# Two gate vectors summed by matrix products, and three masked-matrix steps on GpSimd, in a one-core hybrid layer

## The chip, the core and the metric

One core of a Trainium2 chip runs the whole program. The metric is the device time of one execution in microseconds (us). The core's engines work side by side, each with its own instruction stream: TensorE (PE) for matrix products, VectorE (DVE), ScalarE (ACT) and GpSimd (POOL) for elementwise work. The DMA transfers of this kernel are issued from the queue of SyncE (SP), in order.

## The reference, cut to what matters

The reference is one layer of a generator over 1024 latent tokens of 1024 features, with 256 context tokens. Six vectors of 1024 (shift, scale and gate, twice) come from the conditioning vector:

```python
m = jax.nn.silu(cvec) @ w_ada + b_ada         # 1024 x 6144
sh1, sc1, g1, sh2, sc2, g2 = jnp.split(m, 6)
u = modulate(x, sh1, sc1) @ w_in              # z, x|B|C, dt, f, p
# scan over chunks of 128 tokens, 8 heads, two directions
dt = softplus(dt_raw + dt_bias);  dA = -dt * exp(a_log);  cs = cumsum(dA)
y_diag = einsum("bclhn,bcshn,bhcls,bcshp->bclhp", C, B, exp(segsum(dA)), x * dt)
y = y_diag + (C @ states) * exp(cs)
y = group_rms_norm((y + x * d_skip) * silu(z)) * norm_w
x = LN(alpha * x + g1 * (concat(y, fourier(f), pool(p)) @ w_out))
x = LN(alpha * x + g2 * conv_ffn(modulate(x, sh2, sc2)))
```

Convolution (three taps) and silu go ahead of x, B and C. The term `y_diag` needs, for every chunk and head, the masked matrix of `C B^T` times the decay between two tokens times `dt`, in both directions. A group of four heads shares `B` and `C`; there are two groups.

## The kernel before, in words

Products run in a 32-bit format of TensorE that keeps fewer bits, so each operand is split into a high and a low part, and a product takes three passes.

**Stages.** To 98 us: loads, the layer norm of the tokens, the first shift and scale, and z. From 98 to 228: eight *blocks* of the input projection, in the order B4, C6, B5, C7, x0, x1, x2, x3, 128 columns each, 48 products (L433). Then two blocks for the Fourier part (`pf0`, `pf1`), two for pooling (`pp0`, `pp1`), the scan's outputs by chunk (`Y`, to about 395), the output projection (`pout`, 343 to 467), and the feed-forward net, whose products start at 514 us. The change touches the part from 98 to 395.

**A block** (`block_a`, L553; `block_b`, L573): 48 products and, for B and x, 24 short ones for the context (L444); the convolution, one ACT pass and two on DVE (L548 to L550); silu on ACT (L551); then, in the middle of the next block, transposes on TensorE (`tt`, L578) and copies of them by ACT and DVE (L584, L589), which free PSUM. PSUM is held as two tiles of two banks for the blocks and four of one bank, in rotation, for all else (`tt`, `pc`, `pg`, `pada` and so on).

**The six vectors.** The first shift and scale come early. The other four are made in 32 *pieces* (`ada_piece`, L379): piece i is a load of 128 rows by 1024 columns of `w_ada` (tile `wad`, 512 KB), and DVE multiplies it with the column of silu(c) and adds it to an accumulator of 128x1024 (`aacc`, L389). Pieces 0 to 15 give g1 and sh2, 16 to 31 sc2 and g2. `ada_rows(j)` (L391) sums an accumulator's 128 partitions by four products with a matrix of ones, each into its own 32 rows of one PSUM bank (`pada`, four column groups, L396), copies the result by ACT (`arw`, L398) and stores it. The list `pieces((4, 6, 1, 1, 8, 0, 0, 0)[bi])` says how many pieces come after each block; 12 came before the first.

**The sixteen masked matrices** (`chunk_pre`, L600): one for each chunk and group, in the order of chunks 4, 5, 6, 7, 3, 2, 1, 0 with group 0 and then again with group 1, three after each block from C7 on. The name of a tile has chunk and group: EU30 is chunk 3, group 0, the fifth made. For each:

- TensorE: `pg` = B C^T (L604). DVE: `gt`, both triangles of it (L608).
- DVE: `U` = upper triangle times `dt` (L610, 128x512); then for each of four heads `U` += lower triangle times the other `dt` (L631, 128x128).
- SP: two loads `bc` of the cumulated decays, broadcast over the partitions (L617, from `cs_scratch`); there are two such tiles. POOL (group 0, L619) or ACT (group 1, L623) and ACT again (L628) subtract the own decay; DVE takes the minimum (L630 in group 0, L625 in group 1).
- ACT: the exponential (L632). POOL: times `U` (L633). SP: the store (L634, `m_scratch`).

E and U of a matrix are the two halves of one tile `EU`. Later `Y(i)` (L931) loads a chunk's matrix and states, makes the products, and normalises: two ACT sums of squares (L908), a logarithm and an exponential on two elements a row (`sr`, L911 and L912), a Newton step on DVE (`ssn_t`, L137 to L141), the scaling (L919), transposes on TensorE (`pyt`, L924). A logarithm-and-exponential table set is loaded for it by one instruction of its own (L1009); other table loads go in where an activation needs another set.

**The order.** The calls above say what is computed; a scheduler at build time lays the instructions of each engine into one fixed order, by its own estimates of when operands are ready. An engine never overtakes in that order, and SP's queue doesn't either.

Of the kernel before, what the change touches and what calls it, by code (L numbers as in the profile page):

```python
# [8 lines left out]
F32 = mybir.dt.float32  # L9
F32R = mybir.dt.float32r  # L10
AF = mybir.ActivationFunctionType
ALU = mybir.AluOpType
# [14 lines left out]
def rev_ap(t, hi, n):  # L27
    """Free elements hi, hi-1, ... (n of them) of a two-dimensional tile or AP."""
    a = t[:, hi : hi + 1]
    return bass.AP(a.tensor, a.offset, [list(a.ap[0]), [-1, n]])  # L30
# [3 lines left out]
def hybrid_layer(  # L34
# [16 lines left out]
    def open_psum(na, nb):  # L51
        """PSUM as na tiles of two banks and nb of one."""
# [17 lines left out]
    # Memory that is handed from stage to stage: tags of [P, 1024] words.  # L70
# [11 lines left out]
    def half(tag, name, shape=(P, 512), dt=F32):  # L82
        """One of two tiles of 512 words of a tag of the small pool."""
        return sl.tile(list(shape), dt, tag=tag, name=name, bufs=2)
# [26 lines left out]
    # columns: c 0:8, c_ctx 8:16, conv w 16:40 (tap*8+tile), conv b 40:48, norm_w 48:52, pool_scale 52:54,  # L111
    # b_ada of the first shift 54:62 and scale 62:70
# [21 lines left out]
    def newton(r, v, n, name):  # L134
        """One Newton step of r towards 1/sqrt(v)."""
# [8 lines left out]
    def rstd(var, n, name, scale=1.0):  # L144
        """1/sqrt(var*scale + eps): square root, reciprocal, one Newton step."""
# [8 lines left out]
    def ln_stats(srcs, name):  # L154
        """Mean, 1/deviation and -mean/deviation of the rows of several token tiles, [P, tiles] each."""
# [12 lines left out]
    def modulate(xns, c0, c1, sc, sh, hi, lo, tmps, lo_eng, name, via_act=False):  # L168
        """Transpose token tiles, scale and shift per feature, split into two parts; hi and lo are functions of a range
        of feature tiles."""  # L170
# [33 lines left out]
    def split(raw, hi, lo, eng=None):  # L204
        """hi = raw rounded to float32r, lo = raw - hi (exact)."""
# [3 lines left out]
    # ================= mixer =================  # L209
# [8 lines left out]
    def wblock(c0, name, tags=None):  # L218
        """128 columns of w_in in two parts."""
# [8 lines left out]
    def zload(j, q):  # L228
        """Half the rows of 264 columns: dt and z[0:248], or z[248:512]."""
# [17 lines left out]
    def load_wa(qd):  # L247
        """A quarter of the shift's and of the scale's columns."""
# [28 lines left out]
    hh = [htile("H0", "hh0"), htile("H1", "hh1")]  # L277
    hl = [htile("H2", "hl0"), htile("H3", "hl1")]
    ada1 = sl.tile([P, 2, 8, 2], F32, name="ada1")  # shift or scale, feature tile, latents or context

    def ada_quarter(qd):
        """Two feature tiles of the first shift and scale, for latents and context."""
# [1105 lines left out]
```

## Time and profile before

| | us |
|---|---|
| runs, three | 1237.48, 1238.14, 1640.35; median 1238.14 |
| profiled execution, first to last instruction (span) | 1238.0 |
| TensorE busy in it | 1159.4 (94%) |
| DVE busy | 988.0 (80%) |
| POOL busy | 467.0 (38%) |
| ACT busy | 375.3 (30%) |

The page gives the profiled execution no time of its own beside the span; the span is 0.1 below the median of the runs. Views of the trace list, for a stretch of time, the busy time of each engine; for a group of instructions, their number, total and mean (or shortest, median and longest, in ns); for a wait, who waited, what released it, the total, the number of times and the longest. In a timeline row stand start, duration, engine, line, operation, and in brackets the idle time before it with what ended it. Busy time of an engine that nothing waits for costs nothing; a busy engine that TensorE waits for costs all of it.

### The profile page before, as it was taken

What the parts mean: (1) busy time and instruction counts of PE and PEld (TensorE: products, weight loads), DVE (VectorE), ACT (ScalarE), POOL (GpSimd) and SP (SyncE); (2) the same over time, 40 slices, a digit from 0 to 9 for tenths busy, and PEclk for the clock granted to TensorE, in tenths of its full rate; (3) what the DMA queues carried; (4) which work ended last, traced back from release to release, by engine and by line L of the source; (5) the groups of instructions that cost most, each with busy time, mean ns of one, the idle gap of its engine ahead of it and who ended that gap; (6) DMA issues with size and microseconds to landing.
All of it is one profiled execution on the core that took longest, in us unless ns stands there. A gap on an engine that the chain in (4) does not pass through costs nothing.

```text
span 1238.0 us, 14349 instructions
## 1 busy us (share of the span) xinstructions
PE 1159.4 (94%) x5463; PEld 943.4 (76%) x5463; DVE 988.0 (80%) x1426; ACT 375.3 (30%) x559; POOL 467.0 (38%) x243
## 2 busy tenths in 40 slices
PE   4999998889978998999999999999999999999992
PEld 2798877768756886788888888888888888888881
DVE  4788799999898889798777777777777777778958
ACT  2263566712344132432222212222212122222140
POOL 0010143353352033575353435353434344353254
PEclk9999998989889998999999999999999999999996
DMA  9848555556624011221110212110211112011012
GB/s 314 293 146 298 169 159 173 167 198 219 221 77 171 33 35 51 86 68 51 34 55 31 69 34 68 35 52 34 68 34 50 53 34 69 27 58 52 2 50 119
DMA packets 104637, 122.52 MB, mean 99 GB/s; under 512 B 7006, under 2 KB 83564, under 8 KB 104568
## 3 DMA queue, kind: packets, MB, share of 16 engines
q1 hardware_dynamic: 104567, 121.60, 30.3%
q8 instruction: 43, 0.70, 0.2%
q14 instruction: 27, 0.21, 0.1%
HBM read 106.82 MB, written 14.76 MB: 98 GB/s over the span
## 4 chain that ended last, share of the span: by engine, by line
PE 74%; DVE 16%; DMA 4%; issue 3%; ACT 1%; POOL 1%; SPq 0%; DVEq 0%; ACTq 0%; POOLq 0%
PE pu L1219 37%; PE pdn L1144 16%; PE pout L994 4%; PE px L433 4%; PE pz L332 4%; PE pl L1266 2%; DMA bc<-cs_scratch 1%; PE pu L1180 1%; DVE EU L631 1%; DMA wa<-in_w_ada_dram 1%; DVE pn_st L161 1%; DVE st L696 1%; PE pp L433 1%; DVE xa L1063 1%; PE pd L896 1%
## 5 line engine op out<-in xcount | busy, mean ns | idle before, releaser
L1170 DVE SCALAR_TENSOR_TENSOR cv<-pu,ffc,cv 128x945 f32<-128x945 f32 (+7 forms) x368 | 432.6, 1177 | 20.5 <-ACT cv L1162 10.7
L1219 PE MATMUL pu<-h2h,wul 128*128 128x512 f32 x656 | 205.5, 394 | 0.0
L1219 PE MATMUL pu<-h2h,wuh 128*128 128x512 f32 x656 | 205.2, 394 | 0.0
L1219 PE MATMUL pu<-h2l,wuh 128*128 128x512 f32 x656 | 204.5, 393 | 0.0
L1147 DVE TENSOR_TENSOR xa<-xa,pdn 128x512 f32<-128x512 f32 x128 | 87.4, 683 | 128.9 <-PE pdn L1144 128.6
L207 POOL TENSOR_TENSOR wul<-wur,wuh 128x1024 fp32r<-128x1024 f32 x44 | 106.0, 2409 | 207.9 <-ACT wuh L206 207.9
L1219 PEld LDWEIGHTS pu<-h2h,wuh 128*128 128x128 f32 x656 | 123.3, 188 | 28.9
L1219 PEld LDWEIGHTS pu<-h2l,wuh 128*128 128x128 f32 x656 | 123.3, 188 | 28.6
L1219 PEld LDWEIGHTS pu<-h2h,wul 128*128 128x128 f32 x656 | 123.3, 188 | 27.8
L206 ACT ACTIVATE wuh<-wur 128x1024 fp32r<-128x1024 f32 x44 | 46.3, 1054 | 237.1 <-PE pu L1219 221.5
L1144 PE MATMUL pdn<-wdh,gl 128*128 128x512 f32 x288 | 113.3, 394 | 0.0
L1144 PE MATMUL pdn<-wdl,gh 128*128 128x512 f32 x288 | 113.3, 393 | 0.0
L1144 PE MATMUL pdn<-wdh,gh 128*128 128x512 f32 x288 | 113.1, 393 | 0.0
L1242 POOL TENSOR_TENSOR wdr<-wdr,g2b 128x1024 f32<-128x1024 f32 x22 | 53.0, 2411 | 68.4 <-DMA wdr<-in_ffn_w_down_dram 68.4
L1238 POOL TENSOR_TENSOR cv<-cv,cv 128x1024 f32<-128x1024 f32 (+1 forms) x23 | 53.1, 2308 | 60.5 <-ACT cv L1237 60.4
L207 POOL TENSOR_TENSOR gl<-cv,gh 128x1024 fp32r<-128x1024 f32 (+1 forms) x23 | 53.4, 2320 | 42.3 <-ACT gh L206 42.3
L1144 PEld LDWEIGHTS pdn<-wdh,gh 128*128 128x128 f32 x288 | 54.1, 188 | 12.9
L1144 PEld LDWEIGHTS pdn<-wdh,gl 128*128 128x128 f32 x288 | 54.1, 188 | 12.4
L1144 PEld LDWEIGHTS pdn<-wdl,gh 128*128 128x128 f32 x288 | 54.1, 188 | 12.2
L1162 ACT ACTIVATE cv<-pu,ffc 128x1024 f32<-128x1024 f32 (+3 forms) x46 | 53.1, 1154 | 29.0 <-PE pu L1219 18.8
L1237 ACT ACTIVATE cv<-cv 128x1024 f32<-128x1024 f32 (+1 forms) x23 | 23.5, 1022 | 120.6 <-DVE cv L1170 120.6
L207 POOL TENSOR_TENSOR wdl<-wdr,wdh 128x1024 fp32r<-128x1024 f32 x22 | 52.8, 2414 | 4.7 <-ACT wdh L206 4.7
(348 smaller groups left out, 2142.9 us busy)
## 6 DMA issues: line engine op xcount, KB each, us to landing
wur<-in_ffn_w_up_dram SPq DMA_DIRECT2D x44, 512.0 KB
wad<-in_w_ada_dram SPq DMA_DIRECT2D x32, 512.0 KB
wdr<-in_ffn_w_down_dram SPq DMA_DIRECT2D x22, 512.0 KB
wa<-in_w_ada_dram SPq DMA_DIRECT2D x32, 256.0 KB
bc<-cs_scratch SPq DMA_DIRECT2D x32, 256.0 KB
xr<-in_x_dram SPq DMA_DIRECT2D x8, 512.0 KB
wx_r<-in_w_in_dram SPq DMA_DIRECT2D x8, 512.0 KB
m_scratch<-EU SPq DMA_DIRECT2D x16, 256.0 KB
```

The lines of the kernel that those rows point to most:

```text
L206: S.activation(hi, raw, AF.Identity)
L207: (eng or G).tensor_tensor(lo, raw, hi.bitcast(F32), op=ALU.subtract)
L332: TE.matmul(pt[:, j * 512 : j * 512 + ZW], a, b[:, k % 4, :], start=first and i == 0, stop=last and i == 2)
L433: TE.matmul(pt[:, q * 512 : q * 512 + 512], a[:, k, :], b[q][:, k, :], start=k == 0 and i == 0, stop=k == KD - 1 and i == 2)
L994: TE.matmul(pt[:, nb * 512 : nb * 512 + 512], u, v[:, nb * 512 : nb * 512 + 512], start=first and i == 0, stop=last and i == 2)
L1144: TE.matmul(pt, u_, v_[:, s], start=i == 0, stop=i == n - 1)
L1147: V.tensor_tensor(xa[t][:, s], xa[t][:, s], pt, op=ALU.add)
L1162: S.activation(acc[:, a * 64 : b * 64], pt[:, a * 64 : b * 64], AF.Identity, bias=ffc[:, 396 + ct : 397 + ct], scale=ffc[:, 176 + ct : 177 ...
L1170: last = V.scalar_tensor_tensor(dst, pv[:, r0 + dy : r1 + dy, c0 + dx : c1 + dx], ffc[:, w * 44 + ct : w * 44 + ct + 1], dst, op0=ALU.mult ...
L1219: TE.matmul(pt[:, q * 512 : q * 512 + 512], a[:, k, :], b[q][:, k, :], start=k == 0 and j == 0, stop=k == KD - 1 and j == 2)
L1238: G.tensor_tensor(acc[:, s], acc[:, s], acc_v[:, s], op=ALU.mult)
L1242: G.tensor_tensor(raw, raw, g2b, op=ALU.mult)
```

## The change

**First**, pieces 16 to 31 (j = 1) are no longer accumulated on DVE. Two loaded pieces with the same rows are multiplied at once on TensorE: four products of 32 columns (silu(c) of these rows, for both vectors and padding) with 512 columns, one in each column group, accumulating over the eight pairs in one PSUM bank `pada1`, which stays taken from the first pair to `ada_rows(1)`. The bias is loaded into row 0 of each group of a tile `abias`; DVE adds it when the sum is read. The pieces follow the blocks as 4, 6, 4, 6, and `ada_rows(1)` stands in block x0 instead of x2. **Second**, in `chunk_pre` the product with `dt` is made by GpSimd: `U` as before, `ub` for the lower triangle in one operation, and their sum. `gt` has two buffers. **Third**, the builder reserves less memory for dynamic DMA. The diff removes comments and docstrings besides, so line numbers move.

```diff
     def ada_piece(i):
         j, kk, q = i // 16, (i % 16) // 2, i % 2
         o = 2048 + j * 2048 + q * 1024
-        if i % 16 < 2:
+        if j == 0 and i < 2:
             aacc[j, q] = qt(f"q{6 + q}", f"aacc{j}{q}")
             G.memset(aacc[j, q], 0.0)
             nc.sync.dma_start(aacc[j, q][0:1, :], b_ada[0:1, o : o + 1024])
         t = qt(ptags[i], f"wad{i}")
         nc.sync.dma_start(t, w_ada[kk * P : (kk + 1) * P, o : o + 1024])
-        av = aacc[j, q][:]
-        V.scalar_tensor_tensor(av, t, sil[:, kk, 0:1], av, op0=ALU.mult, op1=ALU.add)
+        if j == 0:
+            av = aacc[j, q][:]
+            V.scalar_tensor_tensor(av, t, sil[:, kk, 0:1], av, op0=ALU.mult, op1=ALU.add)
+            return
+        if kk == 0:
+            aacc[j, q] = t
+            if q == 0:
+                aacc["bias"] = sl.tile([P, 512], F32, name="abias")
+                G.memset(aacc["bias"], 0.0)
+                for b in range(4):
+                    nc.sync.dma_start(aacc["bias"][32 * b : 32 * b + 1, :], b_ada[0:1, o + b * 512 : o + b * 512 + 512])
+                aacc["sum"] = psb("pada1")
+        aacc[j, q] = t
+        if q == 1:
+            for b in range(4):
+                TE.matmul(aacc["sum"][32 * b : 32 * b + 32, :], sil[:, kk, :],
+                          aacc[j, b // 2][:, (b % 2) * 512 : (b % 2) * 512 + 512], start=kk == 0, stop=kk == KD - 1)
 
     def ada_rows(j):
         assert npiece[0] >= 16 * (j + 1)
-        pt = psb(f"pada{j}")
         arw = half("xw", f"arw{j}")
-        for b in range(4):
-            TE.matmul(pt[32 * b : 32 * b + 32, :], ones[:, 0:32], aacc[j, b // 2][:, (b % 2) * 512 : (b % 2) * 512 + 512],
-                      start=True, stop=True)
-        S.copy(arw, pt)
+        if j == 0:
+            pt = psb(f"pada{j}")
+            for b in range(4):
+                TE.matmul(pt[32 * b : 32 * b + 32, :], ones[:, 0:32],
+                          aacc[j, b // 2][:, (b % 2) * 512 : (b % 2) * 512 + 512], start=True, stop=True)
+            S.copy(arw, pt)
+        else:
+            V.tensor_tensor(arw, aacc["sum"], aacc["bias"], op=ALU.add)
...
     def chunk_pre(ch, g):
...
-        gt = sl.tile([P, 2, P], F32, tag="gt", name=f"gt{ch}{g}")
+        gt = sl.tile([P, 2, P], F32, tag="gt", name=f"gt{ch}{g}", bufs=2)
         V.tensor_tensor(gt, pg[:, 0:P].unsqueeze(1).broadcast_to([P, 2, P]), t12, op=ALU.mult)
         f = g * 8
-        V.tensor_tensor(U, gt[:, 0, :].unsqueeze(1).broadcast_to([P, 4, P]),
+        G.tensor_tensor(U, gt[:, 0, :].unsqueeze(1).broadcast_to([P, 4, P]),
                         dtv[:, ch, f : f + 4].unsqueeze(2).broadcast_to([P, 4, P]), op=ALU.mult)
+        ub = sl.tile([P, 4, P], F32, tag="ub", name=f"ub{ch}{g}", bufs=2)
+        G.tensor_tensor(ub, gt[:, 1, :].unsqueeze(1).broadcast_to([P, 4, P]),
+                        dtv[:, ch, f + 4 : f + 8].unsqueeze(2).broadcast_to([P, 4, P]), op=ALU.mult)
         for h in range(4):
...
-            V.scalar_tensor_tensor(U[:, h, :], gt[:, 1, :], dtv[:, ch, b : b + 1], U[:, h, :], op0=ALU.mult, op1=ALU.add)
+        G.tensor_tensor(U, U, ub, op=ALU.add)
         S.activation(E, E, AF.Exp)
         G.tensor_tensor(U, U, E, op=ALU.mult)
...
-        if bi in (1, 6):
+        if bi in (1, 4):
             mids[3].append(lambda: ada_rows(bi // 4))
...
-        pieces((4, 6, 1, 1, 8, 0, 0, 0)[bi])
+        pieces((4, 6, 4, 6, 0, 0, 0, 0)[bi])
...
+    nc = _bacc.Bacc("TRN2", target_bir_lowering=False, num_devices=1, dynamic_dma_scratch_size=1024)
```

With other work to lay out, the scheduler orders three engines differently in places. Names carry a number at their end that tells buffers apart.

SP's queue during block x0, where the stores of the first three matrices (EU40, EU50, EU60) and the `bc` loads of the following ones are issued. Before:

```order
L617 DMA bc700_1707<-cs_scratch 128x2x256
L634 DMA m_scratch<-EU40_1535 128x512
L222 DMA wx3_r_1988<-in_w_in_dram 128x8x128
L617 DMA bc702_1715<-cs_scratch 128x2x256
L634 DMA m_scratch<-EU50_1560 128x512
L634 DMA m_scratch<-EU60_1585 128x512
L617 DMA bc300_1732<-cs_scratch 128x2x256
L617 DMA bc302_1740<-cs_scratch 128x2x256
L634 DMA m_scratch<-EU70_1703 128x512
L617 DMA bc200_1757<-cs_scratch 128x2x256
```

Now:

```order
L640 DMA bc702_1759<-cs_scratch 128x2x256
L222 DMA wx3_r_2002<-in_w_in_dram 128x8x128
L657 DMA m_scratch<-EU40_1555 128x512
L657 DMA m_scratch<-EU50_1579 128x512
L420 DMA ada_scratch<-arw1_1704 1x512
L657 DMA m_scratch<-EU60_1603 128x512
L420 DMA ada_scratch<-arw1_1704 1x512 x3
L640 DMA bc300_1777<-cs_scratch 128x2x256
L640 DMA bc302_1783<-cs_scratch 128x2x256
L640 DMA bc200_1801<-cs_scratch 128x2x256
L640 DMA bc202_1807<-cs_scratch 128x2x256
L640 DMA bc100_1938<-cs_scratch 128x2x256
```

The loads for the fifth, sixth and seventh matrix now come in one run, all behind the first three stores and the store of the second gate sums; the loads of the fifth stand behind the third store in both. The store of the fourth matrix follows them instead of dividing them.

DVE around the convolution of block x0 (`cv0`; its four rows of L549 and L550 before are L569 and L570 now). Before:

```order
L610 TENSOR_TENSOR EU60_1585<-gt60_1586,dtv_1067 128x512
L549 SCALAR_TENSOR_TENSOR cv0_1666<-px0_1617,col_94,cv0_1666 128x1023
L631 SCALAR_TENSOR_TENSOR EU60_1585<-gt60_1586,dtv_1067,EU60_1585 128x128 x4
L550 SCALAR_TENSOR_TENSOR cv0_1666<-px0_1617,col_94,cv0_1666 128x1023
L549 SCALAR_TENSOR_TENSOR cvc0_1696<-pc0_1667,col_94,cvc0_1696 128x255
```

Now, with the copies of the transposes of x0 at the end:

```order
L653 TENSOR_TENSOR EU30_1771<-EU30_1771,bc300_1777 128x256
L653 TENSOR_TENSOR EU30_1771<-EU30_1771,bc302_1783 128x256
L569 SCALAR_TENSOR_TENSOR cv0_1710<-px0_1655,col_94,cv0_1710 128x1023
L653 TENSOR_TENSOR EU20_1795<-EU20_1795,bc200_1801 128x256
L570 SCALAR_TENSOR_TENSOR cv0_1710<-px0_1655,col_94,cv0_1710 128x1023
...
L653 TENSOR_TENSOR EU10_1932<-EU10_1932,bc100_1938 128x256
L653 TENSOR_TENSOR EU10_1932<-EU10_1932,bc102_1944 128x256
L604 COPY xt1_1871<-tt00_1860 128x2x128
L614 COPY xtc_1874<-ttc0_1879 128x2x128
L604 COPY xt3_1873<-tt01_1861 128x2x128
```

The minima of the fifth matrix (EU30) stood behind x0's convolution and now stand ahead of it, and those of the seventh (EU10) ahead of the copies of x0's transposes.

ACT at the last silu, that of block x3 (`cv3`). Before:

```order
L551 ACT_TABLE_LOAD
L551 ACTIVATE cv3_2255<-cv3_2255 128x1024
L551 ACTIVATE cvc3_2285<-cvc3_2285 128x256
...
L632 ACT_TABLE_LOAD
L632 ACTIVATE EU31_2292<-EU31_2292 128x512
L1009 ACT_TABLE_LOAD
```

Now, with the first chunk's normalisation, which had L911 and L912 side by side before:

```order
L1032 ACT_TABLE_LOAD
...
L571 ACT_TABLE_LOAD
L571 ACTIVATE cv3_2255<-cv3_2255 128x1024
...
L655 ACT_TABLE_LOAD
L655 ACTIVATE EU21_2354<-EU21_2354 128x512
...
L934 ACT_TABLE_LOAD
L934 ACTIVATE sr4_2805<-ss4_2802,epsc_97 128x2
L935 ACT_TABLE_LOAD
L935 ACTIVATE sr4_2805<-sr4_2805 128x2
```

The load of the table set for logarithm and exponential (L1009, now L1032) has moved from behind the last silu to ahead of it, and each of the eight chunks now has two table loads in its normalisation; the whole listing of ACT has 40 table loads instead of 24.

More of the change, by code (lines that the diff above doesn't have):

```diff
@@ L1371 @@
     from concourse.bass_utils import run_bass_kernel_spmd as _run
-    nc = _bacc.Bacc("TRN2", target_bir_lowering=False, num_devices=1)
+    nc = _bacc.Bacc("TRN2", target_bir_lowering=False, num_devices=1, dynamic_dma_scratch_size=1024)
     arrays, args = {}, []
```

## Prediction

> **What bounds the kernel now.** I read the page first (engine shares, the chain that ended last), then busy time by stretches, then the waits of the stretch that the change touches, then the start of each projection block on TensorE.
>
> ```profile
> span 1238.0 us, 14349 instructions
> PE 74%; DVE 16%; DMA 4%; issue 3%; ACT 1%; POOL 1%; SPq 0%; DVEq 0%; ACTq 0%; POOLq 0%
> ```
>
> TensorE carries the whole program; DVE comes next with 16% of the chain. The second view shows where. Its columns are stretch, length, then busy us of PE, PEld, DVE, ACT and POOL, the granted clock, the DMA share and GB/s.
>
> ```profile
> 125.00:170.00 45.00, 45.00 (x230) 37.05 (x229) 37.67 (x53) 26.33 (x39) 12.86 (x12) 1.00 0.61 188
> 150.00:290.00 140.00, 126.39 (x616) 104.04 (x615) 131.53 (x251) 70.26 (x127) 59.10 (x52) 0.95 0.57 180
> 180.00:190.00 10.00, 6.41 (x34) 5.53 (x33) 8.91 (x16) 3.85 (x10) 6.34 (x5) 0.82 0.54 161
> 190.00:200.00 10.00, 9.71 (x46) 8.32 (x46) 8.03 (x15) 5.72 (x12) 3.08 (x4) 0.84 0.54 159
> 260.00:270.00 10.00, 6.84 (x27) 5.31 (x26) 9.94 (x28) 1.91 (x5) 3.66 (x3) 0.75 0.41 137
> 270.00:280.00 10.00, 8.88 (x36) 7.05 (x36) 7.61 (x11) 1.53 (x2) 6.18 (x5) 0.91 0.46 157
> ```
>
> From 125 to 170 PE has no gap. From 150 to 290, where the masked matrices are made, PE is idle for 13.6 us (140 less 126.39), DVE is 94% busy and POOL 42%. The lowered clock costs some more: 18% of 6.41, 16% of 9.71, 25% of 6.84 and 9% of 8.88 make 5.2 us. So a DVE with nothing to do there could give back at most about 19 us of 1238; 2% of the time (25 us, about what a measurement of this kernel can tell from no change) is out of reach from this stage.
>
> The third view is the waits: engine, line, releaser, us in total, times, longest.
>
> ```profile
> SPq L634 <- POOL EU L633: 39.1, 15, 5.0
> POOL EU L619 <- DMA bc<-cs_scratch: 35.9, 11, 8.3
> ```
>
> This is a ring: SP's queue stands at the store of a masked matrix until POOL's multiplication L633 is done, the next `bc` load is behind it in that queue, and POOL waits for that load at L619. Today the ring has slack, since POOL is 42% busy. Where TensorE's blocks start:
>
> ```profile
> 156.97 0.72 PE L433 MATMUL px<-hh,wx_h 128*128 128x512 f32 x2
> 171.60 0.71 PE L433 MATMUL px<-hh,wx_h 128*128 128x512 f32 x2
> 193.20 0.73 PE L433 MATMUL px<-hh,wx_h 128*128 128x512 f32 x2
> L433 PE MATMUL pp<-hh,wp_h x24: 388/396/582, 276.3 to 307.7; 128*128 128x512 f32 x24
> ```
>
> x0, x1 and x2 start at 157.0, 171.6 and 193.2, pp0 at 276.3. An undisturbed block is 14.6 us (x0 to x1).
>
> **The change part by part.** Prices:
>
> ```profile
> L389 DVE SCALAR_TENSOR_TENSOR aacc<-wad,sil,aacc 128x1024 f32<-128x1024 f32 x29 | 37.5, 1311 | 3.2 <-DMA wad<-in_w_ada_dram 3.2
> L610 DVE TENSOR_TENSOR EU<-gt,dtv 128x512 f32<-128x512 f32 x16 | 14.4, 898 | 0.1
> L631 DVE SCALAR_TENSOR_TENSOR EU<-gt,dtv,EU 128x128 f32<-128x128 f32 x64 | 23.7, 409 | 0.1
> L633 POOL TENSOR_TENSOR EU<-EU 128x512 f32<-128x512 f32 x16 | 23.5, 1469 | 30.4 <-ACT EU L632 17.8 <-issue 10.0 <-DVE EU L631 2.5
> L633 POOL TENSOR_TENSOR EU<-EU x16: 1279/1297/2206, 165.2 to 269.3; 128x512 f32<-128x512 f32 x16
> L669 POOL TENSOR_TENSOR xw<-xt,wdec x14: 1037/1145/2017, 246.4 to 282.3; 128x512 f32<-128x512 f32 x14
> L619 POOL TENSOR_TENSOR EU<-bc,ncs x16: 612/640/1995, 143.5 to 206.1; 128x256 f32<-128x256 f32 x16
> 129.05 1.00 PE pada L396 x8
> 187.64 0.58 PE L444 MATMUL pc<-hch,wx_h 128*128 128x256 f32 x1 [3.59 <-DVE gt L608]
> ```
>
> *DVE* loses 16 x 1.31 = 21.0 us of L389, 14.4 of L610 and 23.7 of L631: 59 us, nearly all between 130 and 290.
>
> *PE* gains eight groups of four column-group products. The one group that the trace shows (pada, eight records) took 1.0 us; eight of them less the one dropped make +7 us: three near 130, two near 147, three behind the `pg` products ahead of x0. PE has no gap there, so none is hidden: x0 starts at about 165. Bounds 0 (if a later gap takes them up) and 7. The sum also holds one of the four one-bank PSUM tiles until DVE has added the bias, at about 165. The last row shows the dearest wait of PE for such a tile, 3.6 us until DVE had read the `pg` in it, but that was with DVE full; from 130 to 165 DVE loses work, so I take nothing, bounds 0 and 3.6.
>
> *The bias and the sum* go from an ACT copy to a DVE addition on as many elements, and one memset and four small loads move to before 100 us, where SP only queues weights: nothing. Issuing pieces 23 to 31 earlier puts more 512 KB loads into 140 to 165, ahead of the `bc` loads of the second and third matrix; POOL then waits at L619, but its new work starts only at 162, so that too is nothing. The smaller DMA scratch frees memory and costs nothing: the page lists no queue that would use it.
>
> *POOL* gains three 128x512 operations for each of the 16 matrices (8 chunks, 2 groups). No row shows these forms. Two have a broadcast operand, as L669 has (1.145 median), one adds two full tiles, as L633 multiplies them (1.297). Bounds 1.145 and the mean of L633, 1.47; I walk with 1.28, that row's shortest, since the two broadcast forms are nearer to L669. That is 61 us more, and per matrix two L619 and four big operations, 2 x 0.64 + 4 x 1.28 = 6.4 us. Three matrices go with one block: 19.2 us of POOL against 14.6 of PE. So the slack is gone, and POOL sets the pace of the x blocks if anything waits for it. The order listing says that something does: on DVE, x0's convolution stands behind the two minima of the fifth matrix (EU30); the copies that free PSUM ahead of x2 stand behind both minima of the seventh (EU10); and x3's convolution behind those of the thirteenth (EU31). On SP, `bc` of the fifth is behind the stores of the first three.
>
> ```profile
> 156.44 4.13 DMA bc<-cs_scratch
> 184.12 0.33 SPq L634 DMA_DIRECT2D m_scratch<-EU  x1
> 184.56 0.37 SPq L617 DMA_DIRECT2D bc<-cs_scratch  x1
> 172.10 1.27 DVE L549 SCALAR_TENSOR_TENSOR cv<-px,col,cv 128x1023 f32<-128x1023 f32 x1
> 134.87 1.28 ACT L551 ACT_TABLE_LOAD   x1 [2.03 <-DVE cT L550]
> 136.16 1.06 ACT L551 ACTIVATE cT<-cT 128x1024 f32<-128x1024 f32 x1
> ```
>
> The walk, which holds PE's 7 us too: POOL starts batch one at 162 (the `gt` tiles follow `pg` at about 161.5). Twelve big operations and two L619 take 16.6: third multiplication done at 178.8. Store and load issue (0.33 + 0.37) and 4 us for landing: `bc` of the fifth matrix at 183.5. Two L619 and a minimum: 185. Two convolution passes and what stands between, 3 us; table load and silu, 2.3: x0's transposes at about 191. Batch two starts on POOL when its `gt` are made, 189.5; eleven big operations and two L619 later (204.9) the copies ahead of x2 may go, and x2 starts at 207 instead of 193.2, 14 us late. The blocks behind it keep that distance (pp0 at 290 against 276): the last batches hold fewer matrices to a block. With the broadcast forms at 1.145, some 16 of them on this path, 2 us come off. **Term one: +12 us**, with bounds -12 (DVE was all that held PE: 19 back, 7 paid) and +25 (1.47 for the 48 big operations of four batches, 0.19 x 48 = 9 more, and the 3.6 of the PSUM tile).
>
> *The table loads.* The diff doesn't name this. Before, the order has the load of the logarithm-and-exponential set (L1009) behind the last silu. Now it stands ahead of it, silu throws it out, and every chunk's Ln and Exp of the group norm (L911, L912) reload: 16 loads of 1.28 us, 20.5 us on ACT between 297 and 395.
>
> ```profile
> 238.27 1.28 ACT L1009 ACT_TABLE_LOAD   x1
> L912 ACT ACTIVATE sr<-sr x8: 188/204/223, 300.1 to 394.3; 128x2 f32<-128x2 f32 x8
> 300.08 0.20 ACT L912 ACTIVATE sr<-sr 128x2 f32<-128x2 f32 x1
> 300.44 0.15 DVE L137 TENSOR_TENSOR ssn_t<-sr 128x2 f32<-128x2 f32 x1
> 320.09 0.16 DVE L137 TENSOR_TENSOR ssn_t<-sr 128x2 f32<-128x2 f32 x1 [0.39 <-ACT sr L912]
> 381.43 0.16 DVE L137 TENSOR_TENSOR ssn_t<-sr 128x2 f32<-128x2 f32 x1 [0.39 <-ACT sr L912]
> 300.00:310.00 10.00, 10.00 (x57) 8.60 (x56) 9.94 (x16) 5.83 (x16) 4.14 (x2) 1.00 0.44 157
> ```
>
> A pair of loads makes a chunk's `sr` 2.6 us later. The chunks at 320 and 381 wait for `sr` already, with PE's transposition behind DVE: 5.1 us in full. In the first chunk DVE came 0.16 us after `sr`, so it would stand 2.4 us; PE had other work then (10.00 busy in 300 to 310), so of the first two I count half, 2.4. The fourth and sixth have some 1.5 us of DVE work in hand and pay 1 each; the fifth and eighth are covered by DVE's and PE's own work. **Term two: +9.5 us**, bounds 5.1 and 20.5. The Trainium skill, "ScalarE: Activation LUTs", section "What ACT_TABLE_LOAD costs", gives 2.66 us for a switch, load and drain. By it ACT would pay 42.6 us, and term two would be twice as large, 1269 in all; in the row at 136.16 the activation starts right behind its 1.28 us load, so the trace doesn't bear the drain out.
>
> Sum: 1238.0 + 12 + 9.5 = 1259.5; the median of the runs shown is 0.1 above the span, and I say **1259**. The forecast's own range is 1250 to 1269.
>
> **The rivals.** *R1, DVE's relief wins.* If the convolutions don't wait for POOL because the 59 us let everything arrive earlier, PE runs without gaps: -19 + 7, and 5 for the tables (the lower bound): 1231. For it: DVE's 94%. It decides where a batch of POOL fits into 14.6 us, which takes (14.6 - 6 x 0.64)/12 = 0.90 us an operation, under every row above, or where PE's blocks have enough in hand not to need what POOL holds up. *R2, POOL is absorbed.* It paces nothing though it leaves DVE no gain either, and 2 of PE's 7 us are not taken up by the gaps: 1238 + 2 + 9.5 = 1249. For it: POOL waited up to 8.3 us for the ring's loads, and the longest stop of PE in these blocks was the 3.6 at 187.64.
>
> *R3, the two engines block each other.* DVE operations with two inputs in SBUF stretch beside POOL:
>
> ```profile
> 372.01 2.76 DVE L905 TENSOR_TENSOR y<-y,z 128x512 f32<-128x512 f32 x1
> 317.81 0.69 DVE L905 TENSOR_TENSOR y<-y,z 128x512 f32<-128x512 f32 x1
> 182.87 1.50 DVE L630 TENSOR_TENSOR EU<-EU,bc 128x256 f32<-128x256 f32 x1 [0.51 <-POOL EU L619]
> 189.51 0.42 DVE L630 TENSOR_TENSOR EU<-EU,bc 128x256 f32<-128x256 f32 x1 [0.58 <-ACT bc L628]
> ```
>
> The same L905 took 2.76 and 0.69: 2.07 more. With POOL nearly always busy, the two minima (L630) ahead of each of four convolutions would pay that: 8 x 2.07 = 16.6, and 1276. Against it: L630's own stretched row is only 1.1 above the short one, and there are fewer DVE operations to be hit. The Trainium skill, "SBUF — State Buffer", section "SBUF: two separate sides", calls this pair of ports an exclusive lock held for the whole instruction; these rows agree, as far as a longer duration can.
>
> **How the numbers follow.** F, the forecast, 0.52; R1 0.12 (its bound on POOL's price lies below what the rows show); R2 0.15; R3 0.18; 0.03 for anything dearer, such as a longer stall with a lower clock. The likeliest gives 1259. The range leaves out R1 and the top of R3: 1238 to 1280. Faster by over 2% needs under 1213, which no case reaches: 0.02. Slower by over 2% is above 1263: three tenths of F, R3 and the rest, 0.36. Within 2%: 0.62.
>
> **What would show it.** Right: POOL above 90% from 162 to 250; x0, x2 and pp0 at about 165, 207 and 290; DVE's convolutions or minima waiting for POOL's L619 operation or for `bc`; 16 table loads between 297 and 395, PE's idle time from pp0 to the output products up by about 9; eight groups in pada at 1.0 us. Wrong: x2 starting before 200 (then R1 or R2), a POOL operation with a broadcast operand under 1.1 or over 1.5 us, minima near 2 us (R3), or the table loads filling only waits.

## The result and the profile after

The change made the kernel slower by 4%: 1288.31 us (median of 4 runs, 1286.36 to 1291.04) against 1237.81 us of the kernel before on the same chip, a ratio of 1.041 with a 95% interval of 1.039 to 1.043. The prediction said 1259, range 1238 to 1280. One of the four runs of the kernel before took 1640.35 us, far off the other three, and the ratio leaves it out. The profiled execution has a span of 1288.4 us, 50.4 above that of before. In what follows "after" is the changed kernel; its line numbers are those of the second order listing above.

From the page of after, the chain that ended last:

```profile
PE 70%; DVE 11%; DMA 7%; POOL 5%; issue 4%; ACT 3%; SPq 1%; DVEq 0%; ACTq 0%; POOLq 0%
```

DVE's part of the chain fell from 16% to 11%, as the change makes one expect, but POOL's rose from 1% to 5% and DMA's from 4% to 7%. Where PE's blocks x0, x1, x2, x3 and `pf0` start, in the timeline (first products of each), and below them x3 and `pf0` of before, which the prediction doesn't show:

```profile
163.72 0.50 PE L453 MATMUL px<-hh,wx_h 128*128 128x512 f32 x1
178.37 0.71 PE L453 MATMUL px<-hh,wx_h 128*128 128x512 f32 x2
210.88 0.77 PE L453 MATMUL px<-hh,wx_h 128*128 128x512 f32 x1
230.62 0.48 PE L453 MATMUL px<-hh,wx_h 128*128 128x512 f32 x1
254.22 0.71 PE L453 MATMUL pf<-hh,wf_h 128*128 128x512 f32 x2
```
```profile
212.20 0.71 PE L433 MATMUL px<-hh,wx_h 128*128 128x512 f32 x2
227.47 0.71 PE L433 MATMUL pf<-hh,wf_h 128*128 128x512 f32 x2
```

The products of the tile `pp`, with the first one's start:

```profile
L453 PE MATMUL pp<-hh,wp_h x32: 387/397/632, 313.1 to 360.2; 128*128 128x512 f32 x32
```

Set against before, x0 is 6.8 us late, x1 6.8, x2 17.7, x3 18.4, pf0 26.8, pp0 36.8, the output projection (389.3 against 343.5) 45.8 and the feed-forward products (565.1 against 514.5) 50.6. So 37 us are lost up to pp0, in steps of about 10 (at x2, at pf0 and up to pp0) behind PE's first 7, and 14 behind it. Busy time by stretches, in the columns of before:

```profile
125.00:170.00 45.00, 45.00 (x253) 32.56 (x252) 19.26 (x32) 25.03 (x40) 12.20 (x14) 1.00 0.64 202
150.00:290.00 140.00, 103.16 (x508) 84.35 (x507) 70.92 (x106) 67.41 (x120) 85.03 (x78) 0.88 0.41 124
260.00:270.00 10.00, 0.00 (x0) 0.00 (x0) 4.36 (x8) 7.25 (x14) 1.38 (x2) 0.60 0.41 121
```

PE still has no gap up to 170. From 150 to 290 it is idle for 36.8 us instead of 13.6, in single holes (nothing busy from 260 to 270), at a granted clock of 0.88 instead of 0.95. In that stretch no engine is full: DVE 51% busy (94% before), POOL 61% (42%). An engine that is 61% busy sets the pace only if its work stands in series with that of others. The waits from 98 to 440 name the links:

```profile
POOL EU L642 <- DMA bc<-cs_scratch: 32.2, 8, 7.6
POOL EU L630 <- DVE gt L628: 28.1, 5, 10.2
DVE EU L648 <- ACT EU L646: 21.8, 7, 7.8
DVE EU L653 <- ACT bc L651: 18.8, 7, 6.9
ACT EU L646 <- DMA bc<-cs_scratch: 18.5, 4, 8.2
DVE EU L653 <- POOL EU L642: 15.4, 4, 8.5
DVE ssn_t L137 <- ACT sr L935: 12.8, 6, 3.0
```

POOL waits for loads and for DVE's `gt`. DVE waits for the subtraction of the own decay, on POOL (L642) for group 0 and on ACT (L646) for group 1, and ACT waits for loads, which stand behind POOL's stores in SP's queue: a circle. The last row is the group norm's, behind pp0. The end of one turn of the circle, from the chain of waits between 195 and 262 (start, length, work; shortened):

```profile
206.64 1.23 POOL EU L656
...
207.88 0.33 SPq L657
...
208.31 3.98 DMA bc<-cs_scratch
...
213.18 0.76 DVE EU L653
...
213.96 3.23 DMA bc<-cs_scratch
...
218.73 0.34 DVE gt L628
```

POOL works through a batch of three matrices in one run, which begins at 191.93 and ends at 207.87: I call this run the *burst*. Then the store is issued, a `bc` load lands (3.98), DVE takes its minimum, that frees the tile for the next load (3.23), and only then come the next block's convolution, its `gt`, and the next burst. A turn is burst (16) plus way back (11). Behind the fourth burst, whose next matrices are of group 1, the way back goes over the store and ACT (chain from 254 to 270, shortened; the store is issued at 257.09), and PE's transposes wait for the silu behind it:

```profile
257.53 4.34 DMA bc<-cs_scratch
...
261.95 1.09 ACT EU L646 x3
...
263.05 2.62 DMA bc<-cs_scratch
...
265.68 1.22 ACT cv L568
```
```profile
272.21 1.97 PE L598 MATMUL tt<-mat,cv 128*128 128x128 f32 x8 [12.88 <-ACT cv L571]
```

The first multiplications of the second to fifth burst:

```profile
191.93 1.04 POOL L630 TENSOR_TENSOR EU<-gt,dtv 128x512 f32<-128x512 f32 x1 [2.27 <-DVE gt L628]
219.14 1.04 POOL L630 TENSOR_TENSOR EU<-gt,dtv 128x512 f32<-128x512 f32 x1 [5.49 <-DVE gt L628]
243.31 1.04 POOL L630 TENSOR_TENSOR EU<-gt,dtv 128x512 f32<-128x512 f32 x1 [9.12 <-DVE gt L628]
268.62 1.04 POOL L630 TENSOR_TENSOR EU<-gt,dtv 128x512 f32<-128x512 f32 x1 [10.22 <-DVE gt L628]
```

With the first burst at 162.22 the turns take 29.7, 27.2, 24.2 and 25.3 us; an undisturbed block of PE takes 14.6. Each turn holds one block's convolution; before, the convolutions of x0 to x3 (172.10, 196.03, 210.45, 228.37) stand 23.9, 14.4 and 17.9 us apart, and after (186.96, 214.60, 240.17, 266.92) 27.6, 25.6 and 26.8.

### The profile page after: what moved, and what is told of

It reads as the page before. It is cut to its first block, busy times and chain, and to the rows that moved or that the text cites. A ratio compares the mean times of both kernels' runs of the same rounds, so it can differ in the third digit from the quotient of the medians.

```text
span 1288.4 us, 14413 instructions
## 1 busy us (share of the span) xinstructions
PE 1174.7 (91%) x5519; PEld 951.9 (74%) x5519; DVE 945.1 (73%) x1331; ACT 394.7 (31%) x574; POOL 514.8 (40%) x290
## 3 DMA queue, kind: packets, MB, share of 16 engines
q1 hardware_dynamic: 104571, 121.60, 29.7%
## 4 chain that ended last, share of the span: by engine, by line
PE 70%; DVE 11%; DMA 7%; POOL 5%; issue 4%; ACT 3%; SPq 1%; DVEq 0%; ACTq 0%; POOLq 0%
PE pu L1242 35%; PE pdn L1167 15%; PE pout L1017 4%; DMA bc<-cs_scratch 3%; PE pz L332 3%; PE px L453 2%; PE pl L1289 2%; PE pu L1203 2%; POOL EU L654 1%; POOL ub L633 1%; PE pp L453 1%; DMA wa<-in_w_ada_dram 1%; POOL EU L656 1%; DMA ctxr<-in_ctx_dram 1%; POOL EU L630 1%
```

## The experiments

The theories, as they came up: **S**, POOL's burst stands in series with the next block, so each us of it is a us of the turn. Its rivals: the order of DVE's queue alone (minima ahead of the convolution), the two `bc` tiles, the `bc` loads behind the stores in SP's queue (Q), the ring of four EU tiles (E), or the loads and the order together (L). Ratios are to the kernel before, run on the same chip, with 95% intervals.

### The three parts of the loss

**e1_tables**: after, with the table load put back behind the last silu.

```diff
-        S.activation(acc[:, 0:n], acc[:, 0:n], AF.Silu)
+        silu[0] = S.activation(acc[:, 0:n], acc[:, 0:n], AF.Silu)
...
-    lnexp = nc.scalar.preload_act_table_set("natural_log_exp_and_others")
+    with tc.issue_after(silu[0].ins):
+        lnexp = nc.scalar.preload_act_table_set("natural_log_exp_and_others")
```

> The changed kernel with one ordering edge more: the load of the logarithm-and-exponential set is queued behind the last silu. Nothing else of the order around the x blocks changes. If the 14 reloads in the chunks' normalisation are paid on the path (theory: the part from pp0 to the feed-forward net grew by 13.6 us because of them), the time falls by 11 to 15 us, to 1273 to 1277, with pp0 still starting at about 313. If they are mostly hidden behind DVE's and PE's other work (rival) and that part grew because chunks came late, it falls by under 5, to 1284 or more.

1278.25 us, 1.031 (1.029 to 1.033), 23 table loads instead of 40. The reloads cost 10 us by the medians, 12 by the ratios; the time is a little above what was expected if they are paid, and pp0 stays late (315.2).

**e2_ada_only**: the change without its second part (product with `dt` back on DVE). **e3_pool_only**: the kernel before with the second and third part alone.

```diff
-        G.tensor_tensor(U, gt[:, 0, :].unsqueeze(1).broadcast_to([P, 4, P]),
+        V.tensor_tensor(U, gt[:, 0, :].unsqueeze(1).broadcast_to([P, 4, P]),
...
-        ub = sl.tile([P, 4, P], F32, tag="ub", name=f"ub{ch}{g}", bufs=2)
-        G.tensor_tensor(ub, gt[:, 1, :].unsqueeze(1).broadcast_to([P, 4, P]),
-                        dtv[:, ch, f + 4 : f + 8].unsqueeze(2).broadcast_to([P, 4, P]), op=ALU.mult)
...
+            V.scalar_tensor_tensor(U[:, h, :], gt[:, 1, :], dtv[:, ch, b : b + 1], U[:, h, :], op0=ALU.mult, op1=ALU.add)
-        G.tensor_tensor(U, U, ub, op=ALU.add)
```

> The first part of the change alone: gate sums on TensorE, the masked matrices as in the kernel before (DVE makes U). Theory (the loss comes from the second part, POOL's chain of a batch and the order that it leads to): 1238 plus at most PE's 7 us, less what DVE's 21 us give back: 1230 to 1245, pp0 at 270 to 283. Rival (the products, the held PSUM tile, or the crowded loads of the first part are what delays the blocks): over 1255.

> The second part of the change alone: U made by three POOL operations, gate sums on DVE as before. The scheduler's order is another than in the changed kernel: x0's convolution stands behind the minima of the fourth matrix only, not the fifth, the copies ahead of x2 behind the sixth, and the table load stays behind the last silu. Theory (the order decides how much of POOL's work and of the load round trips the blocks see): 1245 to 1258. Rival (POOL's 51 us more work, wherever DVE stands, are too much for the stage): the block part is as late as in the changed kernel, pp0 above 305, 1270 or more.

e2 took 1251.46, 1.010 (1.008 to 1.011); e3 1266.88, 1.022 (1.020 to 1.024); both have 24 table loads. So the gate vectors cost 1.0% (12 us), POOL 2.2% (27 us) and the reloads 0.8 to 1.0% (10 to 12 us), by the medians and by the ratios of e1; together that is the 4.1% of the change. Both times lie between the theory's range and the rival's. The first part was expected to give something back, as DVE is relieved of 21 us; alone it gave nothing. The third part, the smaller scratch, is in both and was not run alone; two later versions have it with more tiles, at 0.999 of the time before.

### What holds the batches: order, loads, tiles

**e4_pin**: DVE's part of the matrices is ordered behind the convolution of the block.

```diff
-        for f in pre((0, 0, 0, 3, 3, 3, 3, 1)[bi]):
-            f()
+        with tc.issue_after(cvl[0].ins):
+            for f in pre((0, 0, 0, 3, 3, 3, 3, 1)[bi]):
+                f()
```

> The changed kernel with the instructions of each batch of matrices on DVE queued behind the convolution of the block that they were written behind; same instructions, same work on each engine; the table load falls behind the last silu by itself, so that the gain of the first experiment is in it too. Theory (the minima that stand ahead of the convolutions carry POOL's chain into TensorE's path): pp0 back to 276 to 290, 1240 to 1255. Rival (POOL's work itself): pp0 stays above 305, 1268 or more.

**e5_bc4**: four `bc` tiles for two.

```diff
-        return sl.tile(list(shape), dt, tag=tag, name=name, bufs=2)
+        return sl.tile(list(shape), dt, tag=tag, name=name, bufs=4 if tag == "bc" else 2)
```

> The changed kernel with four bc tiles instead of two; POOL's, DVE's and ACT's work is the same, the table loads stay at 40. Ring theory (a batch of matrices waits for the loads that stand behind the stores of the batch before, and for two landings one after the other, because there are two tiles): the second landing of every batch falls away, about 4.5 us in each of five, pp0 at 290 to 298, 1263 to 1272. Rival (POOL's work itself holds the blocks): 1283 or more, pp0 above 308.

e4 took 1265.93, 1.021 (1.019 to 1.023); it has 22 table loads, so it stands 12 below e1. e5 took 1278.02, 1.033 (1.030 to 1.035), 40 loads, 10 below after. Each helps and neither is the whole; both times lie between what the theory and the rival gave. **e7_pin_bc4_tables** has both, with the edit of e1:

> The changed kernel with every remedy of order and buffers together: DVE's instructions of a batch behind the convolution, four bc tiles, the table load behind the last silu; POOL's work is kept. If the single gains add up (10 for the tables, 12 for pinning less its table gain, 10 for the tiles): 1254 to 1260. If the order and the tiles cure the same wait: 1263 to 1268. If it falls to 1240 to 1250, POOL's work was never the limit.

1269.52, 1.026 (1.023 to 1.029): no better than the order alone, and nearest to what was expected if the two cure the same wait. Part of what is left can be read in e5, where `bc` is at hand at this place. POOL and DVE at the end of its second burst:

```profile
204.28 1.18 POOL L642 TENSOR_TENSOR EU<-bc,ncs 128x256 f32<-128x256 f32 x2
204.93 1.15 DVE L653 TENSOR_TENSOR EU<-EU,bc 128x256 f32<-128x256 f32 x2 [11.15 <-POOL EU L642]
206.47 0.80 PE L624 MATMUL pg<-cT,bT 128*128 128x128 f32 x2 [6.23 <-DVE xtc L614]
```

The next matrix's subtraction (L642) doesn't wait for its load there; it stands in POOL's queue behind the burst. DVE's minimum waits 11.15 us for it, the copies that free PSUM stand behind the minimum, and PE's `pg` waits for the copies. With two `bc` tiles the load waits at that place as well; with four, the burst alone is enough to hold DVE. That is group 0. In group 1 ACT subtracts, and there e5 waits for a matrix's tile to be stored:

```profile
224.35 1.28 ACT L646 ACTIVATE EU<-bc,ncs 128x128 f32<-128x128 f32 x4 [3.68 <-DMA m_scratch<-EU]
```

**g1_store_pool_bc4** puts the stores on POOL's own queue, with four `bc` tiles, so that the loads on SP's queue no longer stand behind them (Q).

```diff
-        nc.sync.dma_start(ms[ch][:, g * 512 : g * 512 + 512], U.rearrange("p a b -> p (a b)"))
+        G.dma_start(ms[ch][:, g * 512 : g * 512 + 512], U.rearrange("p a b -> p (a b)"))
```

> The changed kernel with four bc tiles and the stores of the masked matrices issued from POOL's own queue, right behind the multiplication, so that no bc load stands behind a store on SP. POOL's twelve operations a batch and the 40 table loads stay. Theory Q (the loads behind the stores make the delay): pp0 at 280 to 292, 1250 to 1264. Theory S (POOL's burst of some 15.5 us a batch stands in series with DVE's minima, copies and the next gt, whatever the loads do): no better than with four tiles alone, pp0 at 300 or later, 1272 to 1282.

1291.46, 1.044 (1.042 to 1.046), 13 above e5 and above both ranges. In the waits from 98 to 440 DVE stands for POOL's subtraction, and longer than after (15.4):

```profile
DVE EU L653 <- POOL EU L642: 21.8, 4, 9.7
```

And in the timeline of POOL the issue of a store lengthens the burst:

```profile
202.20 0.58 POOL L657 DMA_DIRECT2D m_scratch<-EU  x1
```

Three such issues a burst are 7 us in four. Q as the main cause falls; a smaller share of it can't be read from a run that adds POOL work of its own.

**j2_eu6** gives six EU tiles for four, **j2_eu6_pin** the order of e4 besides:

```diff
-    rings["EU"] = ("EM0", "q12", "EM1", "q13")
+    rings["EU"] = ("EM0", "q12", "EM1", "q13", "eu0", "eu1")
```

> The changed kernel with six EU tiles instead of four; work, two bc tiles, stores and table loads as they were. Theory E (a matrix's tile comes free only when POOL has multiplied and the store has landed, and what fills the next one, ACT's and DVE's part, stands ahead of the convolution, so that POOL's burst and the next block run one after the other): with six tiles the next batch can be filled during the burst, pp0 at 290 to 302, 1265 to 1278. Theory S (the series comes through POOL's own order, whatever the tiles): 1283 or more.

> Six EU tiles and DVE's instructions of a batch behind the convolution (this order has the table load behind the last silu, as in the pinned kernel with four tiles, which ran at 1266). Theory E: 1245 to 1258. Theory S: 1262 or more.

1286.04, 1.039 (1.037 to 1.041), and 1268.36, 1.023 (1.022 to 1.025): within 2 to 3 us of after and e4. So E alone falls too. In the second one's timeline POOL's subtraction comes 8 us after the start of the burst (190.42), behind seven of its operations, and DVE's minimum with it:

```profile
198.30 0.61 POOL L644 TENSOR_TENSOR EU<-bc,ncs 128x256 f32<-128x256 f32 x1
198.95 1.47 DVE L655 TENSOR_TENSOR EU<-EU,bc 128x256 f32<-128x256 f32 x1 [5.74 <-POOL EU L644]
```

In group 1 this run, with two `bc` tiles, waits for loads (ACT's L648 3.07 us for `bc` at 251.74), where e5, with four, waits for the tile. No run has four `bc` tiles and six EU tiles together with POOL's three operations, so how much the two hold jointly in group 1 stays open.

### The burst itself

**g2_u_on_dve**: only `U` goes back to DVE (`G.tensor_tensor(U, gt...)` to `V.tensor_tensor`, one line). It takes 3 x 1.12 us from each burst.

> The changed kernel with the first of the three products (U, the upper triangle times dt) back on DVE; ub and the sum stay on POOL. POOL's burst of three matrices gets shorter by 3 x 1.04 us, DVE gets 3 x 0.67 more. Theory S (burst in series): some 2.5 to 3 us a batch, five batches, 12 to 15 us: 1272 to 1277. Theory Q (loads behind the stores, whose time does not change): the stores come earlier by as much, but only the last of a batch counts: 1278 to 1285. If POOL's work is beside the path: 1286 to 1290.

1277.34, 1.032 (1.030 to 1.034): 11 us less with 40 table loads as after. Four bursts by 3.4 are 13. The time is 0.3 us above the range of S and 0.7 below that of Q, so by itself it hardly separates them; it is 9 below what POOL beside the path would give.

**k1_noub**: e1 with `ub` and the sum left out; the backward direction's part is then missing from the masked matrices.

```diff
-        ub = sl.tile([P, 4, P], F32, tag="ub", name=f"ub{ch}{g}", bufs=2)
-        G.tensor_tensor(ub, gt[:, 1, :].unsqueeze(1).broadcast_to([P, 4, P]),
-                        dtv[:, ch, f + 4 : f + 8].unsqueeze(2).broadcast_to([P, 4, P]), op=ALU.mult)
...
-        G.tensor_tensor(U, U, ub, op=ALU.add)
```

> The change with the table load put back behind the last silu, and with the product of the lower triangle (ub) and its addition left out: the decays of the backward direction are then not in the masked matrices, so the output isn't the reference's. The order of the rest is as in the change with the tables put back, which took 1278. POOL keeps two multiplications a matrix, so a batch's burst is shorter by about 7 us. Theory S (POOL's burst stands in series with the next block): three or four batches give back most of that 7, so 1278 less 28, bounds 20 to 35: 1243 to 1258. Rival L (the blocks wait for the landings of bc and for the order, not for POOL's length): at most 12 come back, 1266 or more. Product of TensorE's added work alone sets the floor near 1245.

1254.8, 1.015 (1.012 to 1.017): 23 us below e1 by the medians, 20 by the ratios. That is in what S expected, at its lower end, and well above the 12 that L allowed. Its stretch of the batches:

```profile
150.00:290.00 140.00, 124.24 (x603) 101.09 (x602) 91.75 (x148) 71.06 (x128) 67.96 (x62) 0.94 0.51 159
```

And, in the timeline, a matrix's two minima between the starts of its second burst (185.38) and its third (206.31):

```profile
191.09 0.97 DVE L652 TENSOR_TENSOR EU<-EU,bc 128x256 f32<-128x256 f32 x1 [1.03 <-POOL EU L641]
194.93 0.43 DVE L652 TENSOR_TENSOR EU<-EU,bc 128x256 f32<-128x256 f32 x1 [2.87 <-POOL EU L641]
```

PE is busy for 124.24 of the 140 us (104.28 in e1), pp0 starts at 288.0 (315.2 in e1), and DVE waits 1.03 and 2.87 us for POOL before these two minima, where e1 has 8.49 and 0.50 in front of the same two. The four bursts, by their first and last operation in the two traces, are shorter by 6.5 to 7.0 us each, 27 in all. The four turns take 21.9, 20.9, 20.9 and 20.7 us against 29.6, 27.2, 24.2 and 25.4 in e1, 22 less: the first two turns give back what their bursts lost (14 us for 13), the other two a little over half (8 for 14). By pp0 it is 27. The scheduler lays the rest out anew where two operations are missing, so not all of this need be the burst's length. The time is 6 us above that of e2 by the ratios, 3 by the medians; e2 has none of the three operations on POOL.

### The gate vectors, with cover

**f2_ada_bc4** is e2 with four `bc` tiles and the tables put back; **f5_ada_pin_bc4** adds the order of e4; **j4_ada_eu6_pin** has six EU tiles and that order, and two `bc` tiles.

> The first part of the change alone, as in the second experiment, with four bc tiles and the table load queued behind the last silu. Of the 12 us that the first part cost alone, 7 are the products on PE. Ring theory: the other 5 come from bc loads that the relieved DVE only reaches earlier, and go with four tiles, with part of PE's old gaps: 1236 to 1246. Rival (the products, the held PSUM tile or the crowded weight loads cost all of it): 1249 to 1253, as before the tiles.

> The first part alone with four tiles, and each batch's DVE instructions queued behind the convolution of the block that they were written behind. If ahead of the convolutions any minimum costs time even with the loads early, this is below the kernel with four tiles alone, 1232 to 1240; if not, the same within 3 us.

> A try for a better kernel: gate sums on TensorE, U on DVE as before, six EU tiles, DVE's instructions of a batch behind the convolution, table load behind the last silu. With four bc tiles instead of the two EU tiles it ran at 1239 with 12 us of idle PE left from 150 to 290. If the tiles were part of those: 1230 to 1236. If DVE and the state chain hold them: 1237 to 1242.

1243.89, 1.005 (1.004 to 1.007); 1239.27, 1.001 (0.999 to 1.003); 1246.15, 1.007 (1.005 to 1.008), the last above both ranges given for it. So the waits for `bc` and the order hold nearly all of the first part's 12 us, and with both mended the time is that of the kernel before. Whether DVE's relief then makes up for PE's seven us was not isolated: that needs the kernel before with the same two remedies, and the nearest, l2 below, has six EU tiles besides and is 0.4% faster. DVE falls from 131.5 busy us to 115.5 in the stretch of f2, PE is idle for 12.0 of 140 there, against 13.6 before.

### Versions of the kernel before

**f3_before_bc4** and **j3_before_eu6**: the kernel before with the smaller scratch and four `bc` tiles, or six EU tiles. **h4_before_mixed**: with four `bc` tiles and the order of e4, and POOL's three operations for the last four matrices only. **l2_before_bc4_eu6_pin**: four `bc` tiles, six EU tiles, and the order of e4, all on DVE.

> The kernel before with the smaller scratch and four bc tiles, nothing else. Ring theory: bc loads were 12% of the chain from 150 to 300, so some of PE's 13.6 us without work there comes back: 1229 to 1236. Rival (DVE, 94% busy there, is what holds PE): 1236 to 1240, no change.

> The kernel before with the smaller scratch and six EU tiles. Its POOL is done with a matrix 1.3 us after the exponential, so the tiles are free early: both theories expect little, 1234 to 1240. A fall under 1232 would say that the tiles bound the kernel before as well.

> A try for a better kernel from what the runs showed: the kernel before with the smaller scratch, four bc tiles, DVE's instructions of a batch pinned behind the convolution, the gate sums on DVE as before, and POOL's three operations for the last four of the sixteen matrices only, made from 230 us on, where DVE is at 59 of 60 us and POOL at 32 of 60. DVE loses 4 x 2.4 us there, POOL gains 4 x 3.4. If DVE holds that stretch, 4 to 8 us below the kernel before: 1230 to 1234. If POOL's operations come into the chain of the states there (they share its queue): 1238 or more.

> The kernel before with the smaller DMA scratch, four bc tiles, six EU tiles, and DVE's part of the masked matrices ordered behind the convolution of the block. Each of the first two alone gave 0.999 of the time before. If the loads, the tiles and the order together hold part of the 13.6 us in which TensorE was idle from 150 to 290, it comes out at 1228 to 1235. If DVE's own work holds it (94% busy there), 1236 to 1240.

0.9991 (0.9977 to 1.0004), 0.9988 (0.9971 to 1.0004), 1.0043 (1.0028 to 1.0059) and 0.9972 (0.9959 to 0.9984; 1234.27 us against 1237.44). Even with four matrices on POOL it is slower, 1243.93 us. The last is the one version that is faster than both kernels beyond its interval, by 0.3%. Its stretch of the batches:

```profile
150.00:290.00 140.00, 128.82 (x650) 106.20 (x648) 137.13 (x261) 67.09 (x121) 59.23 (x51) 0.99 0.62 195
```

pp0 starts 7.2 us earlier than before (269.1 against 276.3), the clock is 0.99, PE is idle for 11.2 us and DVE is at 98%, so DVE's own work is the likeliest holder of what is left there; no run tests it.

## Why the prediction was wrong

**Right.** PE's seven us: the added products of `pada` made x0 start at 163.7 (165 predicted), and the held PSUM tile cost nothing, since PE has no gap to 170. The walk along POOL to x2: third multiplication done at 178.3 (walked 178.8), `bc` of the fifth matrix landed at 183.2 (183.5), x2 at 210.9 (207). The walk had one landing too few: the fifth matrix has two `bc` loads, and the second waited for its tile until 184.8 and landed at 188.3. The prices of the walk were near:

```profile
L654 POOL TENSOR_TENSOR EU<-EU,ub 128x512 f32<-128x512 f32 x16 | 23.7, 1481 | 0.3
L656 POOL TENSOR_TENSOR EU<-EU 128x512 f32<-128x512 f32 x16 | 20.8, 1300 | 0.4
L633 POOL TENSOR_TENSOR ub<-gt,dtv 128x512 f32<-128x512 f32 x16 | 19.0, 1189 | 0.0
L630 POOL TENSOR_TENSOR EU<-gt,dtv 128x512 f32<-128x512 f32 x16 | 17.9, 1118 | 33.3 <-DVE gt L628 28.1 <-DVE f L772 5.1
```

Their mean, 1.27, is the 1.28 that was walked.

**Term two**, the table loads, was right in place and nearly in size: +9.5 was said. From pp0 to the feed-forward products after takes 252.0 us, e1 239.8, before 238.2, so 12 are lost behind pp0; the time of e1 makes it 10. ACT in one chunk after, with both loads:

```profile
361.69 1.28 ACT L934 ACT_TABLE_LOAD   x1
362.98 0.30 ACT L934 ACTIVATE sr<-ss,epsc 128x2 f32<-128x2 f32 x1
363.30 1.28 ACT L935 ACT_TABLE_LOAD   x1
364.59 0.20 ACT L935 ACTIVATE sr<-sr 128x2 f32<-128x2 f32 x1
```

Each activation starts right behind its load. The Trainium skill, "ScalarE: Activation LUTs", section "What ACT_TABLE_LOAD costs", adds a drain of 1.38 us to the load; these rows show none, and what ACT pays in them is the 1.28 us of each load.

**The step that failed** is the end of term one: "The blocks behind it keep that distance (pp0 at 290 against 276): the last batches hold fewer matrices to a block." Three matrices go with each block up to the fourth burst, and the distance held only from x2 to x3 (17.7 and 18.4 us); it grew to 26.8 at pf0 and 36.8 at pp0. The walk followed one turn, from the first burst to the second, and took its 14 us for a stall that is paid once. It is paid again: every turn has POOL's burst of 15 to 16 us and a way back of 9 to 14, in which POOL idles (up to 10.22 us, for `gt`), and the four turns took 106.4 us. POOL was not short of throughput: "POOL above 90% from 162 to 250" was the sign asked for, and it was busy for 57.16 of 88 us, 65%:

```profile
162.00:250.00 88.00, 66.03 (x329) 54.29 (x321) 44.77 (x62) 42.57 (x75) 57.16 (x52) 0.88 0.32 98
```

The next turns, walked by the same rows, would have shown the distance grow: from convolution to convolution the second is 3.7 us longer than before, the third 11.2 (25.6 against 14.4) and the fourth 8.9 (26.8 against 17.9). At pp0 23 us more are missing than predicted, and the shorter bursts of k1 give 27 back there. Even both upper bounds of the prediction, 25 and 20.5 us, make 1283.5, below the 1288 measured.

Why the order, tiles and loads each give 10 or 12 and not more together is shown for group 0: POOL's subtraction for the next matrix stands behind operations of the burst whatever is mended (e5, j2_eu6_pin). For group 1 the traces show a wait for the load or for the tile, and no run mends both. Not separated either is how much of the rest is due to operations that grow longer. **R3** was right that DVE's operations grow longer, and partly wrong in which. The minima ahead of the convolutions never took 2 us more (the longest of them took 1.50), but the short steps of group 1 did stretch, most in e7. Their groups before, after and in e7:

```profile
L625 DVE SCALAR_TENSOR_TENSOR EU<-bc,ncs,EU 128x128 f32<-128x128 f32 x32 | 11.9, 409 | 0.1
```
```profile
L648 DVE SCALAR_TENSOR_TENSOR EU<-bc,ncs,EU 128x128 f32<-128x128 f32 x32 | 18.6, 620 | 21.8 <-ACT EU L646 21.8
```
```profile
L652 DVE SCALAR_TENSOR_TENSOR EU<-bc,ncs,EU 128x128 f32<-128x128 f32 x32 | 25.2, 837 | 3.6 <-ACT EU L650 3.6
```

The total grew by 6.7 us after, and by 13.3 in e7, where the order of e4 lays them beside POOL's burst. That may be one reason that the remedies don't add up; no run measures its share of the path.

**R1** fell with x2, **R2** with it. Both had POOL off PE's path, and R1 had DVE as all that held PE. e2 shows besides that DVE was not all: with 21 us less to do on DVE and POOL unchanged, the kernel lost 12, and its chain from 160 to 270 consists to 35% of landings of `bc`.

## What to carry to other kernels

Before moving work to an engine with time to spare, look where that engine stands in the loop. If the next item needs something that comes behind this engine's last step, be it another step in the same queue (group 0 here) or a load that stands behind its store (group 1), what is added counts as latency of every round, though the engine shows 60% busy: here 22 to 27 of 27 us. So walk at least two rounds, and compare the period (burst plus way back) with the block that should cover it. And compare the built order of every engine, of unrelated ones too: a fifth of this loss was a table load that the scheduler moved.

## What the runs showed of the hardware

- On POOL a 128x512 product with broadcast operands takes 1.04 us at its shortest and one of two full tiles 1.26 to 1.30 (rows above), so the broadcast form is the cheaper one.
- A store issued from POOL's queue takes 0.58 us of POOL.
- A DVE operation of 128x128 with two operands in SBUF went from 0.409 to 0.837 us in the mean beside POOL's bursts.
- The granted clock was 0.60 in the stretch in which PE had no product at all (260 to 270) and 0.50 from 272 to 274, right behind it; the eight transposes that came first took 1.97 us there (row at 272.21) against 1.04 before at a clock of 1.00 (202.65 to 203.69). So this hole cost more than its length.
